# The first token block's projections taken from x times the norm's weights, with 1/rms applied behind PSUM and x^T and weights loaded ahead of x's rows

## The chip, the cores and the metric

One core of one Trainium2 chip runs the whole kernel. The metric is device time in microseconds (us), the median of several executions. TensorE is called PE below, VectorE DVE, ScalarE ACT, GpSimd POOL; SP issues nearly all transfers.

## The reference, cut to what matters

```python
def rms_norm(x, g):
    y = x * rsqrt(mean(x * x, axis=-1) + EPS)      # one factor for each token (row of x)
    return y * g                                   # one weight for each of the 1024 features

h = rms_norm(x, norm_g)                            # x: 1024 tokens x 1024 features, float32
z = h @ w_in                                       # all projections of the three mixers
aq, ak, av, ag, bglu, bg, cq, ck, cv, cg, mg = split(z)
aq = rms_norm(aq per head, q_norm_g); ak = rms_norm(ak per head, k_norm_g)
ya = sliding_window_attention(aq, ak, av) * silu(ag) @ w_o_attn
yb = (conformer_conv(bglu) * silu(bg)) @ w_o_conv
yc = differential_attention(cq, ck, cv) * silu(cg) @ w_o_diff
x + (sigmoid gates times ya, yb, yc, summed) @ w_out
```

The factor 1/rms of a token is the same for all its features, so `h @ w` is also `((x * g) @ w) * (1/rms)`, row by row.

## The kernel before

**Tiles.** x is worked on in eight blocks of 128 tokens (n = 0 to 7). Features stand in eight groups of 128 (k = 0 to 7). Each fp32 operand of a product is held as two fp32r parts, high and low (`hi`, `lo`): ACT copies the value into the high part, DVE subtracts that from the value to get the low part. A product is then three matmuls (`mm3`: high by high, weight-low by high, weight-high by low). So a weight or an h can be used once an ACT copy and a DVE subtraction are done.

**How h of one block is made** (`load_x`, `stat`). The block's rows of x (`in_x`, 512 KB) are loaded, ACT squares and sums them (`sqx`), POOL forms 1/rms (`rs`, two small instructions), ACT puts it on a diagonal (`dg`), and PE spreads it over all partitions with one product (`ss`). The transposed block (`in_xT`, 512 KB) is loaded apart from that; POOL multiplies it by the norm's weights (`gain`, L621, in two halves), DVE multiplies it by `ss` (L658), ACT makes `hhi` (L667) and DVE `hlo` (L668), in halves of four k. For blocks 0 and 3 (`GAIN_ON` "-") DVE does both products at once, in eight instructions (L662).

**Projections of mixer A** (`proj_1`). With p = 0, block n gives 512 columns (`zt`): 8 k by 3 matmuls of 128x512, with weights `w_a1` that come in four parts of 512 KB (w0 to w3, two k in each; ACT L380, DVE L376 split each in halves). ACT evicts 384 of the columns (`zn`); the last 128 are v, kept as high and low parts (`vs`, L756 and L757). Then come the norms of q and k, transposes by PE into the one `tr` bank (`tp`, L790), ACT and DVE copies into `q`, `ql` and `kT`, scores (`s`), softmax, transposes of the probabilities into the same `tr` bank (`tp`, L924), and attention (`o`). Beside them runs the GLU projection of mixer B (`zg`), whose weights come from `in_w_col`; the first two of these are loaded during the start.

**Order.** A planner in the kernel (`Issue`) writes the order of every engine's instructions once, at build time, from costs that it assumes and from ranks. At run time each engine takes its instructions strictly in that order, so whatever stands behind a waiting instruction waits too. If a step changes, the planner may order everything behind it in another way. Raw loads share six buffers of 4 KB a partition (`raw`), which the order also hands out; SP issues loads in order, and a load waits for the last reader of the buffer that it takes. `warm` puts small products on PE that nobody reads, ahead of the first real one.

Of the kernel before, what the change touches and what calls it, by code (L numbers as in the profile page):

```python
# [11 lines left out]
F32 = mybir.dt.float32  # L12
F32R = mybir.dt.float32r
I32 = mybir.dt.int32
AF = mybir.ActivationFunctionType
# [257 lines left out]
def mixer_kernel(ctx: ExitStack, tc: tile.TileContext, xT, x, vecs, w_col, w_a1, w_a2, w_c, w_o, w_out, out):  # L273
# [282 lines left out]
    with tc.tile_pool(name="pa", bufs=2) as pa:  # L556
# [28 lines left out]
        KS, VS, ZN, RQ, QK, PR, PP = {}, {}, {}, {}, {}, {}, {}  # L585
        X = {}

        def load_x(n, rank):

            t = X[n] = dict(rank=rank, gain=[])  # L590
# [34 lines left out]
            s0 = iss.step("d", 1.5, dma_rows, [R["raw"]], rank=rank)  # L625
            s1 = iss.step("a", 1.3, square, [s0], rank=rank)
            s2 = iss.step("p", 1.1, power, [s1], rank=-1)
            t["dgs"] = iss.step("a", 0.36, diagonal, [s2, R["dg"]], rank=-1)
            parts = [slice(0, 4), slice(4, 8)] if n == 0 else [slice(0, 8)]
            for j, ks in enumerate(parts):  # L630
                c = (ks.stop - ks.start) / 8
                s3 = iss.step("d", 1.5 * c, lambda ks=ks: dma(ks), [R["raw"]] if j == 0 else [], rank=rank)
                for a in range(ks.start, ks.stop, 4):
                    if GAIN_ON[n] != "-":
                        t["gain"].append(iss.step(GAIN_ON[n], 1.05, lambda a=a: gain(slice(a, a + 4)), [s3], rank=rank + 0.5, port=True))
                    t["there"] = s3

        def stat(n):
            t = X[n]
# [8 lines left out]
            def post_spread():  # L648
                H[n], last = [], []
                for a in range(2):  # L650
# [15 lines left out]
                    s1 = iss.step("v", 0.69 if t["gain"] else 1.36, scale, t["gain"][a:a + 1] + [t["there"]], rank=t["rank"])  # L666
# [5 lines left out]
                t["oh"].by = [last[0], last[3]]  # L672
                t["held"].by = last

            yield 0.25, spread, (lambda: [t["dgs"], R["pv"]]), post_spread

        def stats():

            for n in ALL:
                yield from stat(n)  # L680

        A1 = []
# [2 lines left out]
        def proj_1(p, n):  # L685
# [3 lines left out]
            per = 2 if p == 0 else 4  # L689
            half, sl = n // 4, slice(n % 4 * P, (n % 4 + 1) * P)  # L690
            z = {}

            def piece(me, k):
# [7 lines left out]
                mm3(z["t"][:, :wz], h_hi[half][:, k, sl], h_lo[half][:, k, sl], part["hi"][:, a], part["lo"][:, a],  # L701
                    k == 0, k == NK - 1)

            def after(k):
                if n not in H or k // per >= len((A1, A2)[p]):
                    return None
                w = (A1, A2)[p][k // per]
                return w["cuts"][k % per % len(w["cuts"])] + H[n][k // 4] + ([R["pj"]] if k == 0 else [])

            def post():  # L710
                t, zt = {}, z["t"]

                def copy():
                    t["zn"] = pa.tile([P, 384], F32, name="zn", tag="zn", bufs=A_ZN)
                    ZN[i] = (t["zn"], R["zn"].take(), s4 if p == 0 else s0)
                    act.copy(t["zn"][:, :w], zt[:, :w])

                def square():
                    t["sqh"] = R["sq"].take()
# [25 lines left out]
                s0 = iss.step("a", 0.14 + w / 1250, copy, [R["zn"]], rank=0)  # L745
# [7 lines left out]
                if p == 0:  # L753
                    vsrc = zt[:, 384:512].rearrange("p (a d) -> p a d", d=64)
                    vt = vs[:, n].rearrange("p (a d) -> p a d", d=64)
                    s5 = iss.step("a", 0.27, lambda: act.copy(vt[:, 0:4:3], vsrc))  # L756
                    s6 = iss.step("v", 0.29, lambda: dve.tensor_tensor(  # L757
                        out=vt[:, 1:3], in0=vsrc, in1=vt[:, 0:4:3].bitcast(F32), op=ALU.subtract), [s5])
                    VS[n] = [s5, s6]
                    z["held"].by = [s0, s5, s6]  # L760

# [1596 lines left out]
```

## Time and profile before

| | |
|---|---|
| median of 3 runs (lowest to highest) | 1042.95 us (1042.88 to 1043.30) |
| the profiled execution's own time | 1043.69 us |
| its span, first to last instruction | 1041.8 us |
| PE busy | 1020.8 us of the span |
| DVE, ACT, POOL busy | 739.3, 551.2, 496.1 us |
| mean granted TensorE clock | 0.995 of full speed |

The profiled execution took 1.9 us more than its span, and 0.74 us more than the median of the runs. PE has something in work nearly all the time, so the places to look at are those few where it waits, and those where its clock is low.

### The profile page before, as it was taken

The numbers are of one execution on the slowest core, as the hardware profiler recorded it, in microseconds if no ns is written. First come the engines' busy times: TensorE is split into PE (matmuls) and PEld (weight loads), VectorE is DVE, ScalarE is ACT, GpSimd is POOL, SyncE is SP. The second block draws the span as 40 slices with busy tenths as digits, with TensorE's granted clock in tenths as the row PEclk, the third lists the DMA queues.
The fourth block names the chain that finished last, engine by engine and source line by source line (L and its number), as shares of the span: only waits on it lengthen the run. The fifth ranks groups of instructions, "written<-read, shape, count | busy, mean of one in ns | idle before, by whom it ended". The sixth has DMA issues, their size and how long they took to land.

```text
span 1041.8 us, 15161 instructions
## 1 busy us (share of the span) xinstructions
PE 1020.8 (98%) x5300; PEld 887.4 (85%) x5300; DVE 739.3 (71%) x1266; ACT 551.2 (53%) x1137; POOL 496.1 (48%) x508
## 2 busy tenths in 40 slices
PE   8989999998999999999999999999999999999998
PEld 6778988888999999998888888888888788778887
DVE  6898889977898878889769565555944686755111
ACT  6677875215767667767357657555356354232000
POOL 4836464113233423334118987786775146765200
PEclk9999999999999999999999999999999999999999
DMA  9613323222220402112175454453345785734421
GB/s 314 209 46 105 119 69 119 102 71 72 62 66 16 147 21 88 66 42 87 66 238 192 152 187 157 152 167 127 91 147 189 237 316 183 248 126 152 141 99 54
DMA packets 80364, 136.47 MB, mean 131 GB/s; under 512 B 7456, under 2 KB 32544, under 8 KB 80288
## 3 DMA queue, kind: packets, MB, share of 16 engines
q1 hardware_dynamic: 80000, 135.30, 39.5%
q8 instruction: 42, 0.69, 0.3%
q14 instruction: 34, 0.28, 0.1%
q10 hardware_dynamic: 288, 0.21, 0.1%
HBM read 93.53 MB, written 41.94 MB: 130 GB/s over the span
## 4 chain that ended last, share of the span: by engine, by line
PE 84%; DVE 6%; POOL 3%; ACT 3%; DMA 2%; issue 2%; SPq 0%; POOLq 0%; DVEq 0%; ACTq 0%
PE zu L1821 14%; PE zv L1821 7%; PE zt L341 5%; PE zt L343 5%; PE zt L342 5%; PE y L341 4%; PE y L342 4%; PE y L343 4%; PE zg L341 4%; PE zg L342 4%; PE zg L343 4%; PE zw L1821 3%; PE s L1300 3%; PE f L343 3%; PE f L341 3%; PE f L342 3%
## 5 line engine op out<-in xcount | busy, mean ns | idle before, releaser
L341 PE MATMUL zt<-wh,hhi 128*128 128x384 f32 (+2 forms) x384 | 135.8, 354 | 0.5 <-ACT sq L1172 0.3
L343 PE MATMUL zt<-wh,hlo 128*128 128x384 f32 (+2 forms) x384 | 131.0, 341 | 2.1 <-DVE hlo L668 2.1
L342 PE MATMUL zt<-wl,hhi 128*128 128x384 f32 (+2 forms) x384 | 130.5, 340 | 0.0
L341 PE MATMUL zg<-hhi,wh 128*128 128x512 f32 x224 | 90.3, 403 | 0.0
L343 PE MATMUL zg<-hhi,wl 128*128 128x512 f32 x224 | 87.8, 392 | 0.0
L342 PE MATMUL zg<-hlo,wh 128*128 128x512 f32 x224 | 87.7, 392 | 0.0
L380 ACT CAST wh<-raw 128x1024 fp32r<-128x1024 f32 (+2 forms) x62 | 57.4, 938 | 51.8 <-DMA raw<-in_w_o 17.9
L1182 POOL TENSOR_SCALAR r<-r 128x4 f32<-128x4 f32 x32 | 11.2, 349 | 148.7 <-DVE r L1177 148.6
L1685 POOL TENSOR_TENSOR wu<-st,wu 128x512 fp32r<-128x512 f32 x52 | 70.5, 1364 | 17.4 <-ACT wu L1682 16.8
L376 POOL TENSOR_TENSOR wl<-raw,wh 128x1024 fp32r<-128x1024 f32 x20 | 50.0, 2501 | 60.4 <-ACT wh L380 60.4
L343 PEld LDWEIGHTS zt<-wh,hlo 128*128 128x128 f32 x384 | 73.3, 191 | 5.8 <-DVE hlo L668 2.9
L341 PEld LDWEIGHTS zt<-wh,hhi 128*128 128x128 f32 x384 | 73.7, 192 | 4.0 <-ACT hhi L667 0.8
L342 PEld LDWEIGHTS zt<-wl,hhi 128*128 128x128 f32 x384 | 73.7, 192 | 2.5
L2252 DVE SCALAR_TENSOR_TENSOR yt<-f,yt 128x512 f32<-128x512 f32 (+1 forms) x17 | 11.2, 660 | 72.4 <-PE f L343 72.4
L1328 ACT ACTIVATE pr<-s,sm 128x128 f32<-128x128 f32 (+7 forms) x64 | 47.4, 744 | 17.4 <-DVE sm L1321 12.7
L1321 DVE CUSTOM_DVE_ANT_0 s<-s,mrow,r 128x128 f32<-128x128 f32 (+7 forms) x64 | 51.7, 822 | 6.1 <-PE s L1300 3.2
L341 PE MATMUL y<-oh,wh 128*128 128x512 f32 x128 | 50.2, 392 | 1.2 <-DVE zt L1800 1.2
L341 PE MATMUL f<-wh,mh 128*128 128x512 f32 (+1 forms) x136 | 51.3, 377 | 0.0
L343 PE MATMUL f<-wh,ml 128*128 128x512 f32 (+1 forms) x136 | 51.3, 377 | 0.0
L342 PE MATMUL f<-wl,mh 128*128 128x512 f32 (+1 forms) x136 | 51.3, 377 | 0.0
L342 PE MATMUL y<-ol,wh 128*128 128x512 f32 x128 | 50.1, 391 | 1.1 <-DVE ol L1587 1.1
L1696 POOL TENSOR_TENSOR st<-raw 128x512 f32<-128x512 f32 x28 | 38.2, 1363 | 26.9 <-DMA raw<-in_w_col 26.9
(307 smaller groups left out, 3196.4 us busy)
## 6 DMA issues: line engine op xcount, KB each, us to landing
raw<-in_w_col SPq DMA_DIRECT2D x44, 512.0 KB, 4.2
oG<-zt SPq DMA_DIRECT2D x60, 256.0 KB, 4.2
yt<-oG SPq DMA_DIRECT2D x32, 256.0 KB, 3.6
raw<-in_w_c SPq DMA_DIRECT2D x16, 384.0 KB, 3.5
raw<-in_w_o SPq DMA_DIRECT2D x12, 512.0 KB, 4.1
raw<-in_x SPq DMA_DIRECT2D x8, 512.0 KB, 4.8
oA<-ob SPq DMA_DIRECT2D x16, 256.0 KB, 2.3
oT<-ts SPq DMA_DIRECT2D x16, 256.0 KB, 2.1
```

Source lines behind the costliest of these rows:

```text
L341: pe.matmul(o, lh, rh, start=start, stop=False)
L342: pe.matmul(o, lh, rl, start=False, stop=False)
L343: pe.matmul(o, ll, rh, start=False, stop=stop)
L376: (dve if on == "v" else pool).tensor_tensor(out=t["lo"][:, cs], in0=t["src"][:, cs], in1=t["hi"][:, cs].bitcast(F32), op=ALU.subtract)
L380: s1 = iss.step("a", 0.14 + m / 1200, lambda cs=cs: act.copy(t["hi"][:, cs], t["src"][:, cs]), [s0], rank=rank)
L1182: pool.tensor_scalar(out=t["r"], in0=t["r"], scalar1=EPS, scalar2=None, op0=ALU.add)
L1300: pe.matmul(s[m_][:, jj * 256:(jj + 1) * 256], q[x][:, m_ * 256 + b * P:m_ * 256 + (b + 1) * P], k["kk"][:, m_ * 256:(m_ + 1) * 256], star ...
L1321: dve.tensor_tensor_reduce(out=s[m_][:, :N], in0=s[m_][:, :N], in1=mrow[:, T - N:], scale=NQ[i, b]["r2"][:, 4 + m_:5 + m_], scalar=-NEG, o ...
L1328: act.activation(pr[m_][:, :N], s[m_][:, :N], AF.Exp, bias=t["sm"][:, m_:m_ + 1], scale=-1.0, accum_out=t["su"][:, m_:m_ + 1])
L1685: s2 = iss.step(lo_on, 1.33 if lo_on == "p" else 0.7, lambda: eng.tensor_tensor(out=x["t"][:, 512:], in0=get(), in1=x["t"][:, :512].bitcas ...
L1696: se.tensor_tensor(out=t[nm], in0=x(), in1=y(), op=op)
L1821: pe.matmul(o, l, r, start=bool(start) and k == 0 and i == 0, stop=k == 3 and i == 2, skip_group_check=True)
```

## The change

For the blocks in `AS_IS` (block 0 alone) the projection's left operand is no longer h but the block's x^T times the norm's weights, split into `xh` (ACT) and `xl` (DVE). The factor 1/rms is applied where the products leave PSUM: ACT's copy to `zn` and to v's high part takes it as its scale, and DVE's v-low subtraction becomes one instruction that multiplies and subtracts. h of block 0 is still made, later, for the GLU projection. `GAIN_ON` moves block 0's product with the weights from DVE to POOL. `LOADS` writes out the order of the loads: x^T of block 0, w0, w1, all of block 1, w2, w3, then the rows of block 0. `STATS` puts the spreading product of block 1 ahead of that of block 0.

```diff
-W_AT = {0: (0, 1), 1: (2, 3)}
-LO_ON, GAIN_ON = "vvvvvvvv", "-pp-pppp"
+STATS = (1, 0, 2, 3, 4, 5, 6, 7)
+AS_IS = (0,)
+LOADS = ("x0", "w0", "w1", "b1", "w2", "w3", "r0", "b2", "b3", "b4", "b5", "b6", "b7")
+LO_ON, GAIN_ON = "vvvvvvvv", "ppp-pppp"
...
+            def split(ks):
+
+                if ks.start == 0:
+                    t["xh"], t["xl"] = (pa.tile([P, 1024], F32R, name=nm, tag="wg", bufs=4).rearrange("p (k t) -> p k t", t=P)
+                                        for nm in ("xh", "xl"))
...
+                act.copy(t["xh"][:, ks], t["x"][:, ks])
+
+            def rest(ks):
+                dve.tensor_tensor(out=t["xl"][:, ks], in0=t["x"][:, ks], in1=t["xh"][:, ks].bitcast(F32), op=ALU.subtract)
...
+                    if n in AS_IS:
+                        s4 = iss.step("a", 0.62, lambda ks=ks: split(ks), [t["gain"][-1], Room(R["wg"], 2)] if j == 0 else [t["gain"][-1]], rank=0)
+                        s5 = iss.step("v", 0.69, lambda ks=ks: rest(ks), [s4], rank=0, port=True)
+                        t["parts"].append([s4, s5])
...
-            for n in ALL:
+            for n in STATS:
                 yield from stat(n)
...
+                xh, xl = (X[n]["xh"][:, k], X[n]["xl"][:, k]) if as_is else (h_hi[half][:, k, sl], h_lo[half][:, k, sl])
...
-                    act.copy(t["zn"][:, :w], zt[:, :w])
+                    if as_is:
+                        act.activation(t["zn"][:, :w], zt[:, :w], AF.Copy, scale=X[n]["rs"][:, 0:1])
+                    else:
+                        act.copy(t["zn"][:, :w], zt[:, :w])
...
+                        if as_is:
+                            dve.scalar_tensor_tensor(out=vt[:, 1:3], in0=vsrc, scalar=X[n]["rs"][:, 0:1], in1=hi,
+                                                     op0=ALU.mult, op1=ALU.subtract)
...
-            for n in ALL:
-                load_x(n, 0 if n < X_NEAR else X_RANK)
-                if n in W_AT:
-                    A1.extend(load_part(w_a1[kp], 1024, "w", rank=0, lo_on=W_LO[kp], cuts=len(W_LO[kp])) for kp in W_AT[n])
-                if n == 1:
+            for what, n in LOADS:
+                n = int(n)
+                if what == "w":
+                    A1.append(load_part(w_a1[n], 1024, "w", rank=0, lo_on=W_LO[n], cuts=len(W_LO[n])))
+                else:
+                    load_x(n, 0 if n < X_NEAR else X_RANK, "rx" if what == "b" else what)
+                if (what, n) == ("b", 1):
                     c0 = iss.step("v", 1.3, consts, [At(C_AT)], rank=C_RANK)
```

Three places in the order of the instructions. The first is SP's queue at the start of the program, before the change (raw_133 is x's rows of block 0, raw_164 those of block 1, raw_228 those of block 2):

```order
L596 DMA raw_133<-in_x 128x1024
L617 DMA raw_137<-in_xT 128x4x128 x2
L368 DMA raw_144<-in_w_a1 128x1024
L368 DMA raw_155<-in_w_a1 128x1024
L596 DMA raw_164<-in_x 128x1024
L617 DMA raw_191<-in_xT 128x8x128
L368 DMA raw_203<-in_w_a1 128x1024
L368 DMA raw_219<-in_w_a1 128x1024
L596 DMA raw_228<-in_x 128x1024
L617 DMA raw_246<-in_xT 128x8x128
```

The same place with the change (raw_218 is the rows of block 0, raw_236 those of block 2):

```order
L619 DMA raw_133<-in_xT 128x4x128 x2
L370 DMA raw_138<-in_w_a1 128x1024
L370 DMA raw_147<-in_w_a1 128x1024
L598 DMA raw_159<-in_x 128x1024
L619 DMA raw_167<-in_xT 128x8x128
L370 DMA raw_179<-in_w_a1 128x1024
L370 DMA raw_194<-in_w_a1 128x1024
L598 DMA raw_218<-in_x 128x1024
L598 DMA raw_236<-in_x 128x1024
L619 DMA raw_254<-in_xT 128x8x128
```

One load of 512 KB, the rows of block 0, moves from the head of the queue to behind w3; behind block 2 the order is as it was.

The second place is DVE around the split of the first two GLU weights (`wl` 128x1024), before the change (raw_246 is x^T of block 2, raw_276 of block 3):

```order
L658 TENSOR_TENSOR raw_246<-raw_246,ss_292 128x512
L668 TENSOR_TENSOR hlo0_99<-raw_246,hhi0_97 128x4x128 x2
L730 TENSOR_REDUCE r_346<-sq_331 128x6
L662 SCALAR_TENSOR_TENSOR raw_276<-raw_276,vec_69,ss_348 128x128 x8
L757 TENSOR_TENSOR vs_129<-zt_234,vs_129 128x128
L376 TENSOR_TENSOR wl_325<-raw_322,wh_324 128x1024
L668 TENSOR_TENSOR hlo0_99<-raw_276,hhi0_97 128x4x128
L376 TENSOR_TENSOR wl_345<-raw_342,wh_344 128x1024
L668 TENSOR_TENSOR hlo0_99<-raw_276,hhi0_97 128x4x128
```

The same place with the change (raw_133 is x^T of block 0, raw_254 of block 2, raw_290 of block 3):

```order
L689 TENSOR_TENSOR hlo0_99<-raw_133,hhi0_97 128x4x128 x2
L689 TENSOR_TENSOR hlo0_99<-raw_254,hhi0_97 128x4x128
L679 TENSOR_TENSOR raw_254<-raw_254,ss_329 128x512
L758 TENSOR_REDUCE r_367<-sq_326 128x6
L798 TENSOR_TENSOR vs_129<-zt_279,vs_129 128x128
L683 SCALAR_TENSOR_TENSOR raw_290<-raw_290,vec_69,ss_370 128x128 x8
L378 TENSOR_TENSOR wl_342<-raw_339,wh_341 128x1024
L378 TENSOR_TENSOR wl_356<-raw_353,wh_355 128x1024
L689 TENSOR_TENSOR hlo0_99<-raw_254,hhi0_97 128x4x128
L689 TENSOR_TENSOR hlo0_99<-raw_290,hhi0_97 128x4x128 x2
```

The second half of block 2's `hlo` stood ahead of both GLU weights and now stands behind both; block 0's `hlo` has come in ahead of block 2's.

The third place is PE between two fillings of the `tr` bank, before the change (`tp_781` turns q and k of block 3, `tp_816` the probabilities of block 1):

```order
L984 MATMUL o_776<-pl_753,vs_129 128x256
L790 MATMUL tp_781<-ident_73,zn_609 128x128 x3
L341 MATMUL zg_708<-hhi0_97,wh_324 128x512
L342 MATMUL zg_708<-hlo0_99,wh_324 128x512
L343 MATMUL zg_708<-hhi0_97,wl_325 128x512
L924 MATMUL tp_816<-ident_73,pr_701 128x128 x4
```

With the change the turn that stands ahead of block 1's probabilities is `tp_815`, of block 4:

```order
L1027 MATMUL o_810<-pl_784,vs_129 128x256
L833 MATMUL tp_815<-ident_73,zn_607 128x128 x3
L343 MATMUL zt_792<-wh_149,hhi1_98 128x512
L344 MATMUL zt_792<-wl_150,hhi1_98 128x512
L345 MATMUL zt_792<-wh_149,hlo1_100 128x512
L343 MATMUL zt_792<-wh_149,hhi1_98 128x512
L344 MATMUL zt_792<-wl_150,hhi1_98 128x512
L345 MATMUL zt_792<-wh_149,hlo1_100 128x512
L343 MATMUL zt_792<-wh_181,hhi1_98 128x512
L344 MATMUL zt_792<-wl_182,hhi1_98 128x512
L345 MATMUL zt_792<-wh_181,hlo1_100 128x512
```

Twelve more matmuls of 128x512 follow there before the transposes L967 into `tp_882`, so 21 stand between the two fillings where 3 stood. The reason is that all eight blocks' p = 0 projections now stand ahead of the first GLU matmul, which had been put in ahead of those of blocks 6 and 7.

## Rows read from the trace of the kernel before

**Rows 1.** The page's first part: busy time, share and instructions of each engine.
```profile
PE 1020.8 (98%) x5300; PEld 887.4 (85%) x5300; DVE 739.3 (71%) x1266; ACT 551.2 (53%) x1137; POOL 496.1 (48%) x508
```
**Rows 2.** PE's waits in the whole span, us in total, times, longest.
```profile
PE tp L1230 <- DVE zn L1189: 3.3, 1, 3.3
PE tp L924 <- DVE kT L813: 2.8, 1, 2.8
```
**Rows 3.** Stretches: busy us and instructions of each engine, clock, DMA share, GB/s.
```profile
11.00:27.00 16.00, 13.00 (x55) 9.26 (x54) 13.93 (x30) 11.05 (x23) 8.84 (x12) 1.00 1.02 340
27.00:30.80 3.80, 1.93 (x10) 1.30 (x9) 1.89 (x3) 2.88 (x5) 3.55 (x5) 1.00 0.86 281
30.80:33.80 3.00, 3.00 (x8) 2.31 (x7) 3.00 (x6) 2.03 (x6) 2.92 (x3) 0.50 0.54 185
34.00:65.90 31.90, 31.90 (x170) 26.96 (x168) 28.35 (x61) 24.39 (x68) 18.80 (x26) 1.00 0.37 123
68.80:71.40 2.60, 2.60 (x9) 2.18 (x10) 2.50 (x5) 2.08 (x8) 2.05 (x3) 0.50 0.07 27
72.00:179.00 107.00, 105.57 (x677) 94.15 (x676) 94.12 (x184) 76.91 (x225) 59.17 (x86) 1.00 0.29 96
```
**Rows 4.** Timeline of the start: start us, length, instruction, count, wait before it.
```profile
5.02 0.16 DVE L308 SCALAR_TENSOR_TENSOR gqa<-vec 128x1 f32<-128x1 f32 x1 [5.02 <-DMA vec<-in_vecs]
...
6.27 0.29 DVE L323 TENSOR_REDUCE lams<-lqk 128x2 f32<-128x128 f32 x1
...
8.25 1.14 ACT L380 CAST wh<-raw 128x512 fp32r<-128x512 f32 x2 [0.79 <-DMA raw<-in_w_a]
9.08 2.49 DVE L376 TENSOR_TENSOR wl<-raw,wh 128x512 fp32r<-128x512 f32 x4
...
11.10 1.05 ACT L601 ACTIVATE sqx<-raw 128x1024 bf16<-128x1024 f32 x1
...
11.25 0.50 PE L341 MATMUL zt<-wh,hhi 128*128 128x512 f32 x1
...
13.19 2.04 POOL L621 TENSOR_TENSOR raw<-raw,vec 128x512 f32<-128x512 f32 x2
```
**Rows 5.** The chain that ended last, 0 to 90 us: start us, length, what.
```profile
21.39 6.51 DMA raw<-in_w_col
...
28.87 0.41 ACT dg L611
```
**Rows 6.** DMA issues near 3.29, 10.39 and 22.0 us: count, KB, us to landing.
```profile
raw<-in_x SPq DMA_DIRECT2D x1, 512.0 KB, 7.5
...
raw<-in_w_a SPq DMA_DIRECT2D x1, 512.0 KB, 4.8
...
raw<-in_w_col SPq DMA_DIRECT2D x1, 512.0 KB, 7.2
```
**Rows 7.** Timeline, 29 to 37 us: DVE, and block 2's last matmuls on PE.
```profile
31.34 1.22 DVE L376 TENSOR_TENSOR wl<-raw,wh 128x1024 fp32r<-128x1024 f32 x1
...
32.48 0.68 DVE L668 TENSOR_TENSOR hlo<-raw,hhi 128x512 fp32r<-128x512 f32 x1
...
36.30 0.39 PE L342 MATMUL zt<-wl,hhi 128*128 128x512 f32 x1
36.53 0.39 PE L343 MATMUL zt<-wh,hlo 128*128 128x512 f32 x1
```
**Rows 8.** Timeline, 64 to 70 us: the second filling of the `tr` bank.
```profile
64.98 0.59 ACT L993 COPY ob<-o 128x512 f32<-128x512 f32 x1 [0.94 <-PE o L984]
...
68.00 0.59 DVE L813 TENSOR_TENSOR kT<-tp,kT 64x128 fp32r<-64x128 f32 x2
...
68.74 1.08 PE L924 MATMUL tp<-ident,pr 128*128 128x128 f32 x4 [2.77 <-DVE kT L813]
```
**Rows 9.** Timeline near 44.4 us: a DVE and a POOL instruction side by side.
```profile
44.40 1.04 POOL L621 TENSOR_TENSOR raw<-raw,vec 128x512 f32<-128x512 f32 x1
...
44.50 1.49 DVE L668 TENSOR_TENSOR hlo<-raw,hhi 128x512 fp32r<-128x512 f32 x1
```

More of the change, by code (lines that the diff above doesn't have):

```diff
@@ L586, in mixer_kernel, with load_x @@
         X = {}
-        def load_x(n, rank):
-            t = X[n] = dict(rank=rank, gain=[])
+        def load_x(n, rank, what="rx"):
+            t = X.setdefault(n, dict(rank=rank, gain=[], parts=[]))
             def dma_rows():
@@ L623, in gain @@
                                   op=ALU.mult)
[L625 to L629, printed above, removed]
+            def split(ks):
+                if ks.start == 0:
+                    t["xh"], t["xl"] = (pa.tile([P, 1024], F32R, name=nm, tag="wg", bufs=4).rearrange("p (k t) -> p k t", t=P)
+                                        for nm in ("xh", "xl"))
+                    t["xheld"] = R["wg"].take()
+                    R["wg"].tiles.append(t["xheld"])
+                act.copy(t["xh"][:, ks], t["x"][:, ks])
+            def rest(ks):
+                dve.tensor_tensor(out=t["xl"][:, ks], in0=t["x"][:, ks], in1=t["xh"][:, ks].bitcast(F32), op=ALU.subtract)
+            if "r" in what:
+                s0 = iss.step("d", 1.5, dma_rows, [R["raw"]], rank=rank)
+                s1 = iss.step("a", 1.3, square, [s0], rank=rank)
+                t["rss"] = iss.step("p", 1.1, power, [s1], rank=-1)
+                t["dgs"] = iss.step("a", 0.36, diagonal, [t["rss"], R["dg"]], rank=-1)
+            if "x" not in what:
+                return
+            parts = [slice(0, 4), slice(4, 8)] if n in AS_IS else [slice(0, 8)]
             for j, ks in enumerate(parts):
@@ L664, in scale @@
                                                          in1=t["o"][:, :P], op0=ALU.mult, op1=ALU.mult)
-                    s1 = iss.step("v", 0.69 if t["gain"] else 1.36, scale, t["gain"][a:a + 1] + [t["there"]], rank=t["rank"])
+                    s1 = iss.step("v", 0.69 if t["gain"] else 1.36, scale, t["gain"][a:a + 1] + [t["there"]] + (t["parts"][a] if t["parts"] else []), rank=t["rank"])
                     s2 = iss.step("a", 0.62, lambda hi=hi, ks=ks: act.copy(hi, t["x"][:, ks]), [s1], rank=t["rank"])
@@ L673, in post_spread @@
                 t["held"].by = last
-            yield 0.25, spread, (lambda: [t["dgs"], R["pv"]]), post_spread
+            yield 0.25, spread, (lambda: [t["dgs"], R["pv"]] if "dgs" in t else None), post_spread
         def stats():
-            for n in ALL:
+            for n in STATS:
                 yield from stat(n)
@@ L691, in proj_1 @@
             z = {}
+            as_is = p == 0 and n in AS_IS
             def piece(me, k):
@@ L700, in piece @@
                 a = slice(k % per * wz, (k % per + 1) * wz)
-                mm3(z["t"][:, :wz], h_hi[half][:, k, sl], h_lo[half][:, k, sl], part["hi"][:, a], part["lo"][:, a],
-                    k == 0, k == NK - 1)
+                xh, xl = (X[n]["xh"][:, k], X[n]["xl"][:, k]) if as_is else (h_hi[half][:, k, sl], h_lo[half][:, k, sl])
+                if as_is and k == NK - 1:
+                    X[n]["xheld"].by = [me]
+                mm3(z["t"][:, :wz], xh, xl, part["hi"][:, a], part["lo"][:, a], k == 0, k == NK - 1)
             def after(k):
-                if n not in H or k // per >= len((A1, A2)[p]):
+                x = X[n]["parts"] if as_is else H.get(n)
+                if x is None or k // per >= len((A1, A2)[p]):
                     return None
                 w = (A1, A2)[p][k // per]
-                return w["cuts"][k % per % len(w["cuts"])] + H[n][k // 4] + ([R["pj"]] if k == 0 else [])
+                return w["cuts"][k % per % len(w["cuts"])] + x[k // 4] + ([R["pj"]] if k == 0 else [])
             def post():
@@ L743, in norm @@
                     dve.tensor_tensor(out=zn, in0=zn, in1=t["r2"][:, 4:6].unsqueeze(2).to_broadcast([P, 2, 64]), op=ALU.mult)
-                s0 = iss.step("a", 0.14 + w / 1250, copy, [R["zn"]], rank=0)
+                rs = [X[n]["rss"]] if as_is else []
+                s0 = iss.step("a", 0.14 + w / 1250, copy, [R["zn"], *rs], rank=0)
                 s1 = iss.step(A_SQ[p], 0.1 + w / (1200 if A_SQ[p] == "a" else 450), square, [s0, R["sq"]])
@@ L755, in post, with v_high, v_low @@
                     vt = vs[:, n].rearrange("p (a d) -> p a d", d=64)
-                    s5 = iss.step("a", 0.27, lambda: act.copy(vt[:, 0:4:3], vsrc))
-                    s6 = iss.step("v", 0.29, lambda: dve.tensor_tensor(
-                        out=vt[:, 1:3], in0=vsrc, in1=vt[:, 0:4:3].bitcast(F32), op=ALU.subtract), [s5])
+                    def v_high():
+                        if as_is:
+                            act.activation(vt[:, 0:4:3], vsrc, AF.Copy, scale=X[n]["rs"][:, 0:1])
+                        else:
+                            act.copy(vt[:, 0:4:3], vsrc)
+                    def v_low():
+                        hi = vt[:, 0:4:3].bitcast(F32)
+                        if as_is:
+                            dve.scalar_tensor_tensor(out=vt[:, 1:3], in0=vsrc, scalar=X[n]["rs"][:, 0:1], in1=hi,
+                                                     op0=ALU.mult, op1=ALU.subtract)
+                        else:
+                            dve.tensor_tensor(out=vt[:, 1:3], in0=vsrc, in1=hi, op=ALU.subtract)
+                    s5 = iss.step("a", 0.27, v_high, rs)
+                    s6 = iss.step("v", 0.29, v_low, [s5])
                     VS[n] = [s5, s6]
@@ L1080, in mixer_kernel @@
         with manual:
-            for n in ALL:
-                load_x(n, 0 if n < X_NEAR else X_RANK)
-                if n in W_AT:
-                    A1.extend(load_part(w_a1[kp], 1024, "w", rank=0, lo_on=W_LO[kp], cuts=len(W_LO[kp])) for kp in W_AT[n])
-                if n == 1:
+            for what, n in LOADS:
+                n = int(n)
+                if what == "w":
+                    A1.append(load_part(w_a1[n], 1024, "w", rank=0, lo_on=W_LO[n], cuts=len(W_LO[n])))
+                else:
+                    load_x(n, 0 if n < X_NEAR else X_RANK, "rx" if what == "b" else what)
+                if (what, n) == ("b", 1):
                     c0 = iss.step("v", 1.3, consts, [At(C_AT)], rank=C_RANK)
```

## The prediction

> **What bounds the kernel now.** First the busy time by engine: PE is busy for 1020.8 of 1041.8 us [rows 1], so in the long run only PE counts, and a gain must come out of the 21 us in which it idles, out of stretches with a low clock, or out of the 11 us before its first real matmul at 11.25 us [rows 4]. Then PE's waits: the two longest are single ones, 3.3 us for the first key norms of the next stage and 2.8 us for `kT` [rows 2]; most of what is left lies ahead of 30 us. The stretches show where and at what price: from 11 to 27 us PE is busy for 13.00 of 16 us while the DMA share is 1.02 at 340 GB/s, so the start is fed by transfers; from 27 to 30.8 it is busy for 1.93 of 3.80 us, and the 3.0 us after that run at a granted clock of 0.50, that is 1.2 GHz; the 2.6 us behind the wait for `kT` run at 0.50 too [rows 3]. Half a clock for 3.0 and for 2.6 us costs 1.5 and 1.3 us. From 34 to 65.9 us PE never waits, with DVE at 28.35 of 31.9 us close behind it [rows 3]. Last the chain of waits: before 29 us it runs over the load of the first GLU weight (6.51 us) and the diagonal `dg` queued behind its ACT copy [rows 5]. Block 2's last matmul starts at 36.53 us, 0.23 after the one ahead [rows 7]; with that pitch the block ends at 36.76.
>
> **The change, part by part.** *Rows of x behind w3.* 512 KB at 340 GB/s are 1.5 us [rows 3], by which everything up to w3 lands earlier. w0, for which ACT waited until 8.25 us [rows 4], comes at 6.7; block 1's rows, issued at 3.29 with 7.5 us to landing [rows 6], at 9.3 instead of 10.8.
>
> *Block 0 without 1/rms.* Gone from the path to the first matmul are square, `rs`, `dg` and `ss` of block 0, and DVE's eight instructions L662. In their place: POOL's two halves of `gain` (2.04 us for two [rows 4]) can start when the norm's weights are there, at 5.02 [rows 4], and x^T's first half, with less ahead of it than x had, I estimate at 5.0; halves done at 6.05 and 7.1. ACT's split `xh` is a copy like the weights' (0.57 each half [rows 4]): 6.65. DVE's subtraction `xl` is held beside POOL, as an instruction of 0.68 alone took 1.49 beside L621 [rows 9, 7]: so 7.1 to 7.7. The first high-part weight is there at 7.3, so the first real matmul starts near 7.3, 4 us earlier. That is not the gain: the other products wait for DVE, whose row is now two `xl` and four `wl` (0.62 each [rows 4]), done at 10.85, then the constants, which ran from 5.02 to 6.56 [rows 4] in idle time and now take 1.5 us behind these (12.4). ACT's `dg` of block 1 is queued behind an instruction that needs the constants (13.0); `ss`, the scaling of block 1 and four halves of w2 and w3 (2.49 [rows 4]) follow: 16.6. w3 takes w0's buffer, is issued at 9.6 and lands 4.8 us later [rows 6], in time. Block 0 ends near 17, and block 1, with waits for the second half of its `hlo` and for block 0's late `dg`, near 23.5, where the gap within 27 to 30.8 us [rows 3] shows PE done with it a little after 27.
>
> *Block 2 is where this stops.* Its first half runs until 28. Its second half needs `hlo`, which now stands on DVE behind both GLU weights. The second of these takes the buffer of block 0's x^T, which is now read once more for `hhi` and `hlo` of block 0; that ends near 24.7 (two `hlo` behind a scaling near 23.3). From there 4.8 to 7.2 us to landing [rows 6], an ACT copy of 1.05 (a pass over 1024 columns, as L601 [rows 4]), 1.22 for `wl` and 0.68 for `hlo` [rows 7]: ready at 32.4 to 34.9. Eleven matmuls more are 2.5 us, and the wait ahead of them may lower the clock as at 30.8, for 0 to 1.5 us. Block 2 ends at 34.9 to 38.9; I take the early landing, since the same bytes are ahead of it as before, and half the clock's price: 35.7, so **-1.0** (bounds -1.9 and +2.2).
>
> *The order behind it.* Before, 3 matmuls (0.7 us) stood between the turn of block 3 and the next use of the `tr` bank, while its release took from 64.98 to 68.59 us through ACT and DVE; PE waited for 2.77 us [rows 8]. Now 21 matmuls (4.8 us) stand there. If the release takes the same 3.6 us it is hidden; the wait and the 1.3 us of low clock behind it go: **-4.1** (bounds -4.1 and 0).
>
> *What comes back.* PE then stands some 5 us ahead of where it stood. In the 107 us from 72 to 179 PE waited for 1.4 us with DVE at 94.12 us [rows 3], 88%, and 3.3 us at the change of stage [rows 2]; all of these orders are new. If these waits doubled, 4.7 us would be lost; if DVE keeps up, none. I take **+2.0**. The scale in the evictions of block 0 adds no instruction; split and rest add two ACT copies and two DVE subtractions (2.4 us in all), which lie ahead of 9 us where both engines waited for transfers; without that cover DVE's 1.2 would be paid.
>
> *The clock while block 0 is fed in small pieces.* From 11 to 27 us PE lacked 3.0 of 16 us in pieces and was granted 1.00 throughout; the clock fell behind the gap within 27 to 30.8 us [rows 3]. By these rows block 0, whose gaps I put at 1 us or less, stays at 2.4 GHz. The Trainium skill, "TensorE: Matmul & The Clock Gate", section "Loop structure matters more than you think", holds that a loop with a long wait for data between matmuls lets the array go cold. By that rule block 0 would run at 1.2 GHz; the pieces from 11 to 27 us speak against it for short gaps, the gap at 27 us for it. The sum goes by the rows.
>
> **Sum.** -1.0 - 4.1 + 2.0 = -3.1 us. The profiled execution took 1043.69, 0.74 above the median of 1042.95, so 1040.6 in its terms and 1039.85, say 1039.9, in those of the median. About 0.2% (2.1 us) can be told from no change.
>
> **The rivals.** *The lead is given back* (same). DVE is the second bound, and the change does not relieve it: for block 0 two scalings replace eight smaller instructions, and two `xl` come on top. Then the new orders cost the full 4.7: -1.0 - 4.1 + 4.7 = -0.4, 1042.55. For it: DVE at 88 to 89% of both long stretches [rows 3]; against it: PE did not wait from 34 to 65.9 us under the same load.
>
> *The GLU weights come late* (slower). The one mechanism is `hlo` of block 2 behind `wl` of the second GLU weight. With 7.2 us to landing [rows 6] it comes at 34.9 and block 2 ends at 38.9; DVE, at work on the same row, is late by as much at the next turn, so the wait for `kT` stays: +2.2, 1045.2. It decides when that weight lands after 29.8 us (a loss at all) or 31.9 (over 0.2%). For it: the one load that took 7.2 us is this one, and its buffer comes free later than its issue at 22.0 before. Against it: fewer loads are in flight ahead of it when it is issued.
>
> *The clock stays low in blocks 0 and 1* (same). Block 0's own matmuls hide behind DVE, but block 1's 24 would take 5.5 us more and end at 29, and block 2's first half would end at 34.5 with its second cold behind it, near 39.6: +2.8 - 4.1 + 2.0 = +0.7, 1043.7. For it: three gaps [rows 2, 3] ended in a low clock. Against it: the stretch from 11 to 27 us.
>
> **How the numbers follow.** Forecast 0.50, given back 0.25, late weights 0.17, clock 0.08. So faster 0.50, same 0.33, slower 0.17. The forecast's own range is 1037 to 1041 (its best end: -1.9 - 4.1 = -6.0, 1036.95). For 8 in 10 I go to 1036.9 below, and above through both cases of no change and into part of the late weights, 1044.6.
>
> **What would show it.** First real matmul on PE near 7 us; block 0's last near 17; a PE wait for `hlo` in the middle of block 2, ending at 32 to 33 us, with the second GLU weight landed near 29.5; block 2's end near 35.7; no wait of PE for `kT` between 60 and 75 us; between 72 and 240 us PE idle of 5 to 7 us. I am wrong if block 2 ends after 37 us, if the wait for `kT` or `pr` comes back near 70 us, or if PE loses more than 4 us in excess between 72 and 240 us.

## The result and the profile after

The changed kernel took **1049.84 us** (median of 6 runs, 1046.08 to 1052.75), the kernel before 1042.91 (6 runs, 1042.83 to 1043.31): a ratio of 1.0057, 95% interval 1.0042 to 1.0073. It is slower by 6.9 us where 3.1 us less were forecast. Its single times lie far apart and go with the mean granted clock: 0.997 or 0.998 in the three lowest, 0.991 to 0.993 in the three highest. The profiled execution (1052.33 us) is one of the latter.

Busy time by engine, after; its counterpart is [rows 1]:

```profile
PE 1024.6 (98%) x5300; PEld 889.2 (85%) x5300; DVE 741.1 (71%) x1262; ACT 551.7 (53%) x1139; POOL 499.7 (48%) x510
```

The span grew by 7.6 us to 1049.4. PE is busy for 3.8 us more with the same 5300 matmuls, and idle for 24.8 us where it was 21.0. Of the 3.8 us, 3.0 are lost to the low clock (the sums by slices below).

The start, on PE's timeline, with the wait ahead of an instruction in brackets:

```profile
7.91 0.50 PE L343 MATMUL zt<-wh,xh 128*128 128x512 f32 x1
...
17.57 0.39 PE L343 MATMUL zt<-wh,hhi 128*128 128x512 f32 x1
...
25.43 0.50 PE L343 MATMUL zt<-wh,hhi 128*128 128x512 f32 x1 [1.73 <-ACT hhi L688]
...
33.37 0.50 PE L345 MATMUL zt<-wh,hlo 128*128 128x512 f32 x1 [1.19 <-DVE hlo L689]
...
35.54 0.39 PE L345 MATMUL zt<-wh,hlo 128*128 128x512 f32 x1
...
36.64 0.49 PE L667 MATMUL ss<-dg,onesf 128*128 128x128 f32 x2 [0.71 <-ACT dg L613]
43.30 0.49 PE L667 MATMUL ss<-dg,onesf 128*128 128x128 f32 x2 [0.98 <-ACT dg L613]
53.02 0.49 PE L667 MATMUL ss<-dg,onesf 128*128 128x128 f32 x2 [0.51 <-DVE raw L679]
```

The first real matmul comes at 7.91 us (11.25 in [rows 4]), block 0 is done at 17.57, and block 2's last matmul starts at 35.54 (36.53 in [rows 7]). But three spreading products `ss` now keep PE waiting up to 54 us. The wait of 1.73 us ahead of block 2 has its reason on ACT, which stands for 2.57 us on the load of block 3's rows, squares them, and copies both halves of block 0's `hhi` before the first of block 2's:

```profile
22.68 1.06 ACT L603 ACTIVATE sqx<-raw 128x1024 bf16<-128x1024 f32 x1 [2.57 <-DMA raw<-in_x]
...
23.74 1.64 ACT L688 CAST hhi<-raw 128x512 fp32r<-128x512 f32 x3
```

The stretches, in the columns of [rows 3]:

```profile
7.90:17.60 9.70, 9.48 (x56) 7.98 (x56) 9.02 (x24) 8.00 (x16) 3.16 (x6) 1.00 0.95 348
...
27.60:31.00 3.40, 3.40 (x10) 2.67 (x10) 3.13 (x10) 3.11 (x7) 3.15 (x5) 0.52 0.71 272
...
34.00:65.90 31.90, 29.70 (x152) 24.29 (x150) 27.62 (x59) 22.99 (x65) 21.10 (x28) 1.00 0.47 155
65.90:72.00 6.10, 5.71 (x33) 4.78 (x32) 5.89 (x13) 4.69 (x16) 3.60 (x5) 1.00 0.13 39
72.00:179.00 107.00, 104.39 (x683) 93.63 (x682) 101.07 (x193) 79.28 (x232) 62.48 (x91) 1.00 0.32 104
...
300.00:440.00 140.00, 135.25 (x849) 127.65 (x849) 116.38 (x257) 93.61 (x215) 47.31 (x71) 0.99 0.22 70
```

In the first row, block 0's, some 3.6 of the 9.48 busy us are `warm` products: 28 of the 60 now stand behind the first real matmul, where before all stood ahead of it. So that row shows a full PE, but not a block 0 without gaps.

From 65.9 to 72 us, where the wait for `kT` stood [rows 8], PE lacks only 0.39 us and the clock is full. The last row is the surprise: from 300 to 440 us, in the stage of mixer C, PE is busy for 135.25 of 140 us. The same row of the kernel before:

```profile
300.00:440.00 140.00, 139.22 (x889) 133.25 (x887) 119.33 (x267) 98.83 (x227) 49.13 (x75) 1.00 0.22 69
```

Four microseconds are lost in a stage that the diff does not touch. PE's waits of after between 236 and 440 us say for what (total, times, longest):

```profile
PE tp L1275 <- DVE zn L1234: 3.3, 1, 3.3
PE zg L343 <- ACT sq L1217: 2.9, 2, 1.8
PE zt L343 <- ACT sq L1217: 1.3, 2, 1.0
PE s L1345 <- ACT q L1307: 0.5, 1, 0.5
```

The first was there before [rows 2]; the waits for `sq`, ACT's squares of a projection, are new but for 0.3 us. The places of two of them, ACT's timeline and then PE's:

```profile
302.10 0.48 ACT L1213 COPY zn<-zt 128x384 f32<-128x384 f32 x1 [0.71 <-PE tp L1275]
302.48 0.97 ACT L1293 ACTIVATE q<-tp,gqc 64x256 fp32r<-64x256 f32 x2
303.47 0.74 ACT L1300 CAST kk<-tp 64x256 fp32r<-64x256 f32 x2
304.24 0.82 ACT L1307 CAST q<-q 64x256 fp32r<-64x256 f32 x2
305.07 0.38 ACT L1217 ACTIVATE sq<-zt 128x256 f32<-128x256 f32 x1
...
303.98 0.40 PE L345 MATMUL zg<-hhi,wl 128*128 128x512 f32 x1
305.50 0.51 PE L343 MATMUL zg<-hhi,wh 128*128 128x512 f32 x1 [1.13 <-ACT sq L1217]
```

```profile
371.89 0.95 ACT L1293 ACTIVATE q<-tp,gqc 64x256 fp32r<-64x256 f32 x2
...
374.50 0.48 ACT L1213 COPY zn<-zt 128x384 f32<-128x384 f32 x1
374.87 0.39 ACT L1217 ACTIVATE sq<-zt 128x256 f32<-128x256 f32 x1
...
375.31 0.50 PE L343 MATMUL zg<-hhi,wh 128*128 128x512 f32 x1 [1.77 <-ACT sq L1217]
```

The projections `zt` and `zg` share two PSUM banks, and the square is the last reader of a `zt`, so PE cannot begin the next projection in its bank before it. At 302 us ACT evicts q and k (`q`, `kk`, 2.5 us in all) between the copy and the square of one projection, at 372 us ahead of both. The old order has such a place too (q and k between copy and square at 348 us), and there PE waits only 0.30 us for the square. So it is not the order of ACT alone, but what PE has left to do meanwhile.

To see where time goes in the whole program, this table adds up, over slices of 1 us of the stretches view, PE's idle time and its busy time times (1 - granted clock): us lost since the start.

```
up to us         40     80    240    300    440    800   1020
before         7.83  12.07  16.20  18.92  19.71  20.46  22.82
after          7.46   9.34  15.21  18.54  24.99  25.36  29.52
```

After is 2.7 us ahead at 80 us, 1.0 ahead at 240, 0.4 at 300, and 5.3 behind at 440. Another 1.6 us goes at 918 us, a low clock behind a wait that both kernels have. Around 1020 us the difference is 6.7 of the 7.6 us. The sum counts as work the `warm` products too (9.79 us busy before, 10.29 after), and the longer first matmul behind a wait (0.50 us where those behind it take 0.39), so a lead of 1 us in it is not sure. A plainer measure is one matmul that all kernels have: PE's last `zg` ahead of mixer C's stage starts at 224.51 us before and at 223.95 after, a lead of 0.6 us.

### The profile page after: what moved, and what is told of

It reads as the page before. It is cut to its first block, busy times and chain, and to the rows that moved or that the text cites. A ratio compares the mean times of both kernels' runs of the same rounds, so it can differ in the third digit from the quotient of the medians.

```text
span 1049.4 us, 15144 instructions
## 1 busy us (share of the span) xinstructions
PE 1024.6 (98%) x5300; PEld 889.2 (85%) x5300; DVE 741.1 (71%) x1262; ACT 551.7 (53%) x1139; POOL 499.7 (48%) x510
## 4 chain that ended last, share of the span: by engine, by line
PE 78%; DVE 9%; DMA 5%; ACT 4%; issue 2%; POOL 2%; SPq 0%; POOLq 0%; DVEq 0%; ACTq 0%
PE zu L1866 13%; PE zv L1866 7%; PE zt L343 4%; PE zt L344 4%; PE zt L345 4%; PE y L344 4%; PE y L343 4%; PE y L345 4%; PE zg L343 3%; PE s L1345 3%; PE zg L345 3%; PE zg L344 3%; PE zw L1866 3%; PE f L344 3%; PE f L343 3%; PE f L345 3%
## 5 line engine op out<-in xcount | busy, mean ns | idle before, releaser
L343 PE MATMUL zt<-wh,hhi 128*128 128x384 f32 (+2 forms) x376 | 132.4, 352 | 3.0 <-ACT hhi L688 1.7
L345 PE MATMUL zt<-wh,hlo 128*128 128x384 f32 (+2 forms) x376 | 127.6, 339 | 1.3 <-DVE hlo L689 1.3
L344 PE MATMUL zt<-wl,hhi 128*128 128x384 f32 (+2 forms) x376 | 127.5, 339 | 0.0
L343 PEld LDWEIGHTS zg<-hhi,wh 128*128 128x128 f32 x224 | 42.4, 189 | 11.1 <-ACT sq L1217 3.8
```

The costliest lines, as they stand in the source:

```text
L343: pe.matmul(o, lh, rh, start=start, stop=False)
L344: pe.matmul(o, lh, rl, start=False, stop=False)
L345: pe.matmul(o, ll, rh, start=False, stop=stop)
```

## The experiments

The planner also fills idle time of DVE with the taps of mixer B's convolution (`conv`, instructions `co`, some 0.75 us each). In mixer A's stage it gave DVE 36 taps before the change and 39 after. Behind that the orders part for good: only PE's last 1567 matmuls stand as before. Holding the taps at 36 with the change brings the old order back towards the end of mixer A's stage (PE's last 4272 matmuls, from 186 us on, and DVE's last 890 instructions). So the start and the order behind it can be tried apart. Three theories were set against each other: **R**, the new order of the later stages costs the time; **K**, the granted clock does, whatever the order; **S**, the change itself is slow by what it adds on DVE and POOL.

| | median us (lowest to highest, runs) | ratio to before, 95% |
|---|---|---|
| *before beside e1 to e4* | 1044.46 (1042.01 to 1047.23, 17) | |
| e1, changed, 36 taps | 1044.72 (1042.62 to 1046.90, 12) | 1.0005 (0.9995 to 1.0014) |
| e2, before, later order of after | 1048.26 (1046.66 to 1049.85, 6) | 1.0038 (1.0023 to 1.0053) |
| e3, e1 with the old loads | 1049.83 (1049.38 to 1050.22, 5) | 1.0053 (1.0040 to 1.0066) |
| e4, before, gain on POOL | 1050.49 (1047.27 to 1052.67, 6) | 1.0056 (1.0036 to 1.0076) |
| *before beside e5 to e8* | 1043.87 (1041.36 to 1046.04, 23) | |
| e5, changed, once more | 1048.40 (1045.42 to 1051.06, 7) | 1.0040 (1.0026 to 1.0055) |
| e6, e1, block 0 spread last | 1051.27 (1050.47 to 1051.82, 5) | 1.0069 (1.0056 to 1.0082) |
| e7, changed, 35 taps | 1045.42 (1043.85 to 1048.12, 12) | 1.0017 (1.0007 to 1.0028) |
| e8, changed, 33 taps | 1046.32 (1043.92 to 1049.16, 11) | 1.0027 (1.0014 to 1.0039) |
| *before beside e9 to e12* | 1043.31 (1041.85 to 1046.24, 20) | |
| e9, e1, six taps moved | 1041.23 (1040.47 to 1043.02, 9) | 0.9978 (0.9968 to 0.9988) |
| e10, before, six taps moved | 1042.91 (1040.47 to 1045.18, 12) | 0.9993 (0.9982 to 1.0004) |
| e11, e9, rows of block 0 late | 1058.91 (1057.17 to 1059.99, 4) | 1.0143 (1.0126 to 1.0161) |
| e12, e11, block 0 spread late | 1052.96 (1052.06 to 1055.99, 6) | 1.0092 (1.0077 to 1.0107) |

### e1 and e2: start and later order exchanged

e1 holds the taps of the changed kernel at 36 (a third line, not shown, lifts the limit for the stages behind mixer A's):

```diff
-            if at is not None and self.spared * self.spare.cost < self.spare_rate * (v - self.spare_from):
+            if at is not None and self.spared < self.cap and self.spared * self.spare.cost < self.spare_rate * (v - self.spare_from):
...
-        iss.spare, iss.spare_rate = conv, 10.0
+        iss.spare, iss.spare_rate, iss.cap = conv, 10.0, 36
...
```

> The changed kernel with one number pinned: DVE may take at most 36 of the convolution's taps before mixer C's stage begins, as many as the planner gave it before the change (39 with the change). With that, every engine's order from the end of mixer A's stage on is the order of before. Theory R (the stage behind was ordered anew, and lost there what the start had won): the lead of 1.0 us that the changed kernel's trace still shows at 240 us stays to the end, so 1041.9 us (1040.9 to 1042.9), and PE no longer waits for ACT's squares between 300 and 440 us. Theory K (the loss comes from the granted clock, whatever the order): single times still spread over several us, 1045 to 1052. Theory S (the change itself slows the work, by what it adds beside DVE and POOL): 1046 or more with little spread.

e2 is the kernel before with three taps more at the end of mixer A's stage:

```diff
+        for _ in range(3):
+            conv.issue(iss.free['v'] - 3.0)
         iss.spare_rate, iss.spare_from, iss.spared = TAP_RATE, iss.now, 0
```

> The kernel before, its start untouched, with three more taps of the convolution put on DVE at the end of mixer A's stage. By that every engine's order from there on is the changed kernel's. Theory R: the loss of the later stages comes with the order, 6 us between 242 us and the end, less up to 2 us if the three taps cost nothing where they stand and nothing of the low clock returns: 1047 to 1050 us, with PE waiting for ACT's squares between 300 and 440 us. Theory K or S: within 2 us of before, 1042 to 1045.

PE's waits between 236 and 440 us, two lines of e1:

```profile
PE tp L1275 <- DVE zn L1234: 3.1, 1, 3.1
...
PE zt L343 <- ACT sq L1217: 0.3, 1, 0.3
```

and of e2:

```profile
PE zg L341 <- ACT sq L1174: 2.9, 2, 1.8
...
PE zt L341 <- ACT sq L1174: 0.8, 2, 0.5
```

The waits for `sq` go with the order: away with the old one, though the start is the changed kernel's, and there with the new one, though the start is the old one's, with 2.9 us in total just as in after. So do the times: e2 lands where R put it, and e1 at no difference from before. That is above R's range for e1, which had counted on a lead that lasts. K is out as the main cause: e1 and before spread alike (4.3 and 5.2 us on that chip) and agree. S is out too, since e1 carries the whole change and is the program of e5 below (1.0040) but for the taps and what follows from them. What R missed is that e1's lead does not last: by the sums it is 1.3 us at 240 us, 0.6 at 300, none at 440. By the last `zg` it was only 0.3 us (224.19 by 224.51).

```
up to us         40     80    240    300    440    800   1020
e1             7.49   9.43  14.90  18.33  19.73  20.49  23.27
e2             6.34  12.52  16.15  18.92  23.24  24.29  26.78
```

That matmul and block 2's last one can be read in every trace. Up to 219 us the orders of before, e2 and e10 are the same, and so are those of after, e1, e5, e7, e8 and e9:

| start of a matmul, us | old start: before, e2, e10 | changed start: after, e1, e5, e7, e8, e9 |
|---|---|---|
| block 2's last | 36.53, 34.52, 34.78 | 35.54, 35.92, 35.60, 34.92, 37.47, 36.97 |
| last `zg` ahead of mixer C | 224.51, 225.04, 224.17 | 223.95, 224.19, 223.96, 223.28, 226.16, 223.30 |

So one start scatters by 1 to 3 us from trace to trace (they come from several chips). At the end of block 2 the changed start has no lead at all in the middle of its traces, and ahead of mixer C one of some 0.5 us, below the scatter.

### e3 and e4: parts of the change alone

e3 is e1 with the old loads and the old order of the spreading products:

```diff
-STATS = (1, 0, 2, 3, 4, 5, 6, 7)
+STATS = (0, 1, 2, 3, 4, 5, 6, 7)
-LOADS = ("x0", "w0", "w1", "b1", "w2", "w3", "r0", "b2", "b3", "b4", "b5", "b6", "b7")
+LOADS = ("b0", "w0", "w1", "b1", "w2", "w3", "b2", "b3", "b4", "b5", "b6", "b7")
```

> As e1, but the loads stand in their old order (the rows of block 0 first) and the spreading products too: only the projection of block 0 from x times the norm's weights is left of the change. If the loads' order is what brings block 2's end forward, this one loses most of the lead that e1 has: block 2 ends within 0.5 us of before's 36.76, total 1042 to 1043.5. If leaving out the norm is what brings it, block 2 ends near 35.8 as in the changed kernel, total within 0.5 us of e1.

e4 is the kernel before, 36 taps pinned, with one letter changed:

```diff
-LO_ON, GAIN_ON = "vvvvvvvv", "-pp-pppp"
+LO_ON, GAIN_ON = "vvvvvvvv", "ppp-pppp"
```

> The kernel before with block 0's product with the norm's weights on POOL, and nothing else of the change (36 taps pinned, so the later stages keep their order). DVE is rid of eight instructions of block 0 and gets two in their place. If DVE's work is what holds the start, the first matmul comes no later than before (11.25 us) and block 2 ends up to 1 us earlier: 1041.5 to 1042.5. If transfers hold it, no change within 0.5 us: 1042.4 to 1043.4.

Both expectations failed, on the end of block 2 and on the total. In e3 block 2's last matmul starts at 33.28 us and in e4 at 32.40, 3.3 and 4.1 us before the old kernel's 36.53 [rows 7], yet the kernels end 5.4 and 6.0 us later. What the planner pushed back for that is late next: PE's waits of e3 from 0 to 150 us,

```profile
PE zt L343 <- DVE vs L798: 3.1, 2, 2.9
PE ss L667 <- ACT dg L613: 2.8, 2, 2.1
PE s L890 <- DVE kT L856: 2.4, 1, 2.4
```

and of e4 from 30 to 110 us:

```profile
PE s L847 <- DVE kT L813: 2.4, 1, 2.4
PE ss L646 <- ACT vs L756: 2.1, 1, 2.1
PE zg L341 <- DVE vs L757: 1.4, 1, 1.4
```

So the end of block 2 is no measure of the start: all of mixer A's stage hangs on DVE and ACT, and a block that PE gets early is paid for by the scores and the low part of v. Their last `zg` ahead of mixer C starts at 232.10 and 229.98 us, 7.6 and 5.5 behind before's: all of the loss is made by then.

### e5, e7 and e8: other orders of mixer C's stage

e5 is the changed kernel again. e7 and e8 are e1 with 35 and 33 in place of 36.

> The changed kernel as it is, on the chip of the next three, as the measure for them. Theory R (the later stages' new order costs the time): 1048 to 1051 us, PE waiting for ACT's squares between 300 and 440 us for 3 us or more. Theory K (clock alone): on a chip where the kernel before takes its lower times, 1043 to 1046.

> The changed kernel with 35 taps before mixer C's stage. The order of PE and ACT in that stage is the changed kernel's for most of it, the taps of the convolution stand elsewhere on DVE. Theory R: PE's waits for ACT's squares come back at the same places, 1047 to 1051 us. If it were the taps on DVE that cost the time, and not the order of the others: 1044 to 1046.

> The changed kernel with 33 taps before mixer C's stage: a third order of that stage, equal to the changed kernel's for the first two thirds of it. Theory R as a matter of places: the waits at 305 and 375 us stay as far as the order is the same, 1046 to 1051 us. If 36 taps gave a good order by chance only and others scatter around it, this one may as well come out at 1044 or less.

e5 repeats the loss, and its trace has the same waits: 2.9 and 0.9 us for `sq`. It also settles K: five of its runs have a mean clock of 0.997 or 0.998 and take 1045.42 to 1048.95 us, while the eight runs of before with that clock on that chip take 1041.36 to 1044.05. In e7 they come back as R says (2.9 and 1.2 us), but the time is below R's range, and not for the reason of the taps theory: e7 had lost only 13.91 us at 300 us where e1 had lost 18.33, and 20.02 at 440 where e1 had lost 19.73. The gain came at the change of stage. e7's two lines:

```profile
PE zg L343 <- ACT sq L1217: 2.9, 2, 1.8
PE tp L1275 <- DVE zn L1234: 1.3, 1, 1.3
```

The wait for the first key norms is 1.3 us there and no low clock follows; in e1 it is 3.1 us (3.3 in [rows 2]). e8 has 1.3 us too, its waits for `sq` are there (2.9 and 0.9 us), and its time is in R's range. So neither e7 nor e8 contradicts R; they add a second lever.

### e6: block 0's h made last

```diff
-STATS = (1, 0, 2, 3, 4, 5, 6, 7)
+STATS = (1, 2, 3, 0, 4, 5, 6, 7)
```

> As e1 (36 taps, later stages in the order of before), with the spreading product of block 0 moved behind those of blocks 2 and 3, as h of block 0 is wanted by the GLU projection alone. Both halves of block 2's low part then stand on DVE ahead of the GLU weights, and ACT makes block 2's high part before block 0's. If PE's wait for that high part at 26 us (1.58 us in e1's trace), the low clock behind it (1.7 us) and the wait for the low part are worth what they last, block 2 ends 2 to 4 us before e1's and 1041 us is left; if DVE, which has the same work to do, sets the pace behind block 2, the gain is below 1 us: 1043.7 to 1045 by e1's 1044.7.

Block 2's last matmul starts at 30.39 us, 5.5 us before e1's (35.92), and the kernel is some 6.5 us slower than e1. Waits of e6 from 30 to 150 us:

```profile
PE zt L343 <- DVE vs L798: 3.2, 1, 3.2
...
PE tp L967 <- DVE pl L979: 2.0, 1, 2.0
```

Both ends of the expectation missed: more was lost behind than was won, as in e3 and e4 (the last `zg` ahead of mixer C at 234.22). But e6 shows what the wait ahead of block 2 was made of. With block 0's two copies out of its way, block 2's high part comes right behind ACT's square of block 3's rows, and the wait is 0.90 us where e1 had 1.58:

```profile
24.30 0.50 PE L343 MATMUL zt<-wh,hhi 128*128 128x512 f32 x1 [0.90 <-ACT hhi L688]
```

So ACT's order holds PE up by two copies of some 0.5 us, and the square with the load that it waits for by the rest. How long the wait is in a single trace varies: 1.00 us in e5 and 1.73 in after, which are one program.

### e9 and e10: the change of stage mended

What the wait at the change of stage hangs on is in e1's timelines (DVE, ACT, PE):

```profile
225.54 1.07 DVE L1093 SCALAR_TENSOR_TENSOR ug<-sig,zg 128x512 f32<-128x512 f32 x1
...
230.55 0.48 ACT L1213 COPY zn<-zt 128x384 f32<-128x384 f32 x1 [16.17 <-DMA oU<-ug]
...
240.48 0.47 PE L1275 MATMUL tp<-ident,zn 128*128 128x128 f32 x1 [3.07 <-DVE zn L1234]
```

ACT's first eviction of mixer C waits for the transfer out of `ug`, the GLU's last product, and `ug` stands on DVE behind seven taps, late by 0.96 us against PE's end of `zg` (its last matmul starts at 224.19, 0.39 long). e9 is e1 with 35 taps and the 36th behind `ug`, by which six taps come to stand there (e1 has none):

```diff
-        iss.spare, iss.spare_rate, iss.cap = conv, 10.0, 36
+        iss.spare, iss.spare_rate, iss.cap = conv, 10.0, 35
...
             iss.flush()
+            for _ in range(1):
+                conv.issue(iss.free['v'] - 3.0)
```

> As e1 (later stages in the order of before), but the 36th tap and the five taps behind it stand on DVE behind the last product of the GLU (the one into ug) instead of ahead of it. In the traces that product's transfer out is what mixer C's first eviction on ACT waits for, and with 35 taps (e7) PE waited 1.35 us for the first key norms instead of 3.07 and stood 4.7 us ahead of e1 at 260 us. Theory R, with the change of stage mended: 2 to 4 us below e1 and before, 1041 to 1043 by 1044. If DVE's taps, moved by 4.7 us, only make the next norms late: within 0.5 us of e1.

e10 does the same in the kernel before, where three of the six stood behind `ug` already.

> The same move of six taps in the kernel before, without any of the change. If the move alone brings the gain, it comes here as in e9, 2 us or more below before (1041 to 1042 by 1044), and the change adds nothing; if the change's lead of 1 us at 240 us lasts once the change of stage is mended, e9 is about 1 us below this one.

e9's timelines at the three places:

```profile
223.79 1.10 DVE L1093 SCALAR_TENSOR_TENSOR ug<-sig,zg 128x512 f32<-128x512 f32 x1 [3.78 <-PE zg L345]
...
228.02 0.48 ACT L1215 COPY zn<-zt 128x384 f32<-128x384 f32 x1 [14.53 <-PE zt L345]
...
237.91 0.33 PE L1277 MATMUL tp<-ident,zn 128*128 128x128 f32 x1 [1.38 <-DVE zn L1236]
```

`ug` follows PE at once, ACT's eviction comes 2.53 us earlier, and PE's wait is 1.38 us at a full clock behind it. The profile puts ACT's wait down to PE now, but SP's next load, which waits for the transfer out of `ug`, starts at 227.99 us, so transfer and PE end together there. e9 is faster than the kernel before by 2.1 us by the medians. The move alone (e10) gains 0.4 us, within what can be told. e10 still has the 2.8 us wait for `kT` of the kernel before and a mean clock of 0.993 to 0.998; e9 has neither that wait nor a clock below 0.997. Between e10 and e9 lies the change: 1.7 us by the medians, 0.3 to 2.7 when the runs of both are drawn anew (95%). So the change gains something once the order behind it is held and the change of stage mended; with the order alone held (e1) it gains nothing.

### e11 and e12: rows of block 0 later still

e11 is e9 with `"b2", "r0"` in place of `"r0", ... "b2"` in `LOADS`; e12 also has `STATS = (1, 2, 0, 3, ...)`.

> As e9, with the rows of block 0 loaded behind those of block 2 and its x^T. The start is fed with 512 KB less ahead of block 2, but block 0's 1/rms and with it its eviction come later. If PE's wait for block 2's high part at 26 us comes from ACT's and DVE's work on h of block 0 ahead of it, it stays: within 1 us of e9 up to 72 us. If it comes from the transfer of block 2's rows, block 2 ends 1 to 2 us earlier than in e9.

> As e11, with the spreading product of block 0 behind that of block 2 too, so that ACT and DVE make both halves of block 2's h ahead of block 0's. If order on ACT is what PE waits for at 26 us, that wait (1.6 us) and the low clock behind it (1.7 us) go, and block 2 ends 1.5 to 3 us earlier than in e9; whether this is left at the end depends on the order of mixer A's stage, which the planner writes anew: 1040 to 1047.

Both failed. One line of PE's timeline of e11 and one of e12 show for what:

```profile
30.93 0.76 PE L667 MATMUL ss<-dg,onesf 128*128 128x128 f32 x2 [3.18 <-DVE raw L679]
```

```profile
34.63 0.77 PE L667 MATMUL ss<-dg,onesf 128*128 128x128 f32 x2 [9.04 <-DVE raw L683]
```

A spreading product waits for DVE to have scaled another block with the one before it, and all of PE stands behind it; block 2 starts at 31.61 and 35.69 us. By taking the wait away from one place it was made larger at the next. They say nothing on the wait at 26 us, of which e6 had shown both parts.

## Why the prediction was wrong

**The start, -1.0: right in this trace, and by luck.** First matmul 7.91 (forecast 7.3), block 0's end 17.57 (17), wait for `hlo` in the middle of block 2 ending at 33.37 (32 to 33), block 2's end at 35.77 (35.7). It came by another way than told: the wait of 1.73 us ahead of block 2, for its high part behind block 0's and behind a square that waited for its load, was not foreseen, and the clock fell behind it. Other traces of the same two starts end block 2 as early without the change as with it, so the lead of 1 us is one pair of executions. The clock during block 0 was 1.00, as the rows said, but `warm` products filled its gaps, so the case of a block 0 with gaps was not met. The Trainium skill has in "TensorE: Matmul & The Clock Gate", section "Loop structure matters more than you think", that long waits for data between matmuls let the array go cold. It did here (0.52) behind the wait of 1.73 us, and in e5 it did not behind three waits of 1.00 to 2.05 us between 23 and 34 us. What the runs refuted is what the term was used for: in e3, e4 and e6 block 2 ends 3 to 6 us early and the kernel loses.

**The order behind it, -4.1: half right.** The wait for `kT` and the low clock behind it went as forecast, in all six traces of the changed start. But the step took over that PE never waits from 34 to 65.9 us [rows 3]. It waited for 2.2 of these 31.9 us, mostly for the three spreading products, as ACT's `dg` and DVE's scaling are late. The net at 80 us is 2.7 us, where the first two terms make 5.1.

**What comes back, +2.0: right in size.** From 80 to 240 us after loses 5.9 us and before 4.1: 1.7 us in excess, with DVE busy for 101.07 of the 107 us from 72 to 179 (94.12 before, [rows 3]). At 240 us the lead is 1.0 us by the sums, 0.6 by the last `zg`, instead of 3.1.

**The step that failed** is the sum: it ends at 240 us, and puts all behind that at nothing. The text said that the planner may order everything behind a changed step anew, and counted new orders "between 72 and 240 us" only. Three taps more on DVE were enough for another order of mixer C's stage; there 5.7 us were lost against before from 300 to 440 us (4.0 us of PE idle, 1.7 of low clock behind the wait at 375 us). e1 and e2 show it from both sides. The second step that failed is the -5.1 of the first two terms, of which 2.7 us were there at 80 us and 0.6 at the last `zg` ahead of mixer C, because PE waits where the rows had it never wait (the 2.2 us above). So even with the later order held, e1 gains nothing. None of the rivals had the loss: "late weights" ends on the same side, but the second GLU weight (issued at 25.7, 4.5 to 4.8 us to landing) came at some 30.3, between that rival's marks of 29.8 and 31.9, and block 2 ended where forecast. "The lead is given back" is what e1 shows.

## What to carry to other kernels

Where a planner writes the order, compare the order of all stages before and after, not of the stage that was edited, and price what moved there; pin the rest by its inputs (here one count of taps) before an edit is judged. The early end of one block proves nothing while another engine paces the stage: compare the start of one and the same matmul at the stage's end, in more than one trace of each kernel. And a wait at a change of stage can hang on the last transfer out of the stage before; with the change in place, six small instructions put behind the one that feeds it took the ratio to before from 1.0005 (e1) to 0.9978 (e9).

## What the hardware showed unexpectedly

One and the same wait need not cost the clock. In after PE waits for 1.77 us at 375 us and is then granted 0.59; in e5, the same program, it waits for 1.78 us at the same place and is granted 1.00 (after, then e5):

```profile
375.30:378.70 3.40, 3.39 (x13) 3.11 (x14) 2.87 (x5) 1.82 (x3) 2.47 (x4) 0.59 0.00 0
```

```profile
373.80:377.20 3.40, 3.38 (x20) 2.94 (x21) 2.87 (x5) 1.83 (x3) 2.46 (x4) 1.00 0.00 0
```

PE got 20 instructions done in these 3.4 us where it got 13. So the price of a wait is itself plus a chance of more: each low stretch behind a wait cost 1.5 to 1.7 us in the traces of before and after, and 2.9 us in one case (after, behind the change of stage). It fits that a kernel that waits often spreads more (6.7 us in after, 2.6 in e9), though not every kernel does (e3: 0.8 us); what decides it in a single run was not found.
